# The state of an S5 branch: three elementwise operations that ran on POOL run on DVE

## The chip, the core and the metric

The kernel runs on one core of one Trainium2 chip. A core has a matrix engine (TensorE, here PE, with its weight loads as PEld), a vector engine (VectorE, DVE), a scalar engine (ScalarE, ACT), a general engine (GpSimd, POOL) and a sync engine whose queue issues most of the DMAs (SyncE, SP). Each engine runs its own queue of instructions in order and waits on semaphores of the others. The metric is the device time of one execution in microseconds, here the median of several runs. A profiled execution gives the trace; its times are from the start of its span.

## What is computed

One layer of a hybrid block on x of 1024 tokens by 1024 channels, in float32. After an RMSNorm, one combined projection makes the inputs of all branches. Branch A is the S5 state space: 64 groups of 16 channels with 64 complex states each. Branch B is sparse attention: an indexer scores the keys, each query keeps the 256 best, and attention runs over those. Both are gated and merged, then follow an output projection, a SwiGLU and a last norm. Cut to what matters here:

```python
lb_re = mag * jnp.cos(ai * dt)
lb_im = mag * jnp.sin(ai * dt)
...
x_re = f_re * bu_re - f_im * bu_im
x_im = f_re * bu_im + f_im * bu_re
a_s_re = jnp.broadcast_to(lb_re, shp)
a_s_im = jnp.broadcast_to(lb_im, shp)
...
_, _, h_re, h_im = lax.associative_scan(combine, (a_s_re, a_s_im, x_re, x_im), axis=0)
y = (jnp.einsum('lbgp,gcp->blgc', h_re, c_re.astype(f32))
     - jnp.einsum('lbgp,gcp->blgc', h_im, c_im.astype(f32))
     + d_skip.astype(f32) * uf)
```

## The kernel before

**Precision.** Matmuls run on float32 data split in a high and a low part (`whi`, `wlo`, `h_hi`, `h_lo`); a product is three matmuls (L209 to L211). So each weight tile needs a cast (L89, on ACT or, for most gate weights, POOL) and a subtraction on DVE (L90), and many results are split in the same way (L192, L193).

**S5 in chunks.** Time is cut in pieces of 8 steps, so 128 chunks. Within a chunk a Toeplitz matrix gives the output; between chunks only the state is carried. A complex rotation per chunk is taken out of the state beforehand, so that the rest is a real recurrence with a positive factor `r8`, which DVE's scan instruction runs along the 128 chunks. Afterwards the rotation is put back. `s5_batch` handles one of 8 batches of 8 groups; `s5_half` half a batch, so there are 16 halves. A half has 128 partitions (64 states, real parts above, imaginary below) and 4 groups x 128 chunks = 512 elements in each. Its steps:

- POOL makes `bt` and `ct` (L544 to L550), PE transposes `bt` into `s5t` (L554), ACT copies it into `ba` (L555), PE makes the Toeplitz blocks `s5k` (L558), and `kt` goes by DMA into `toep`.
- ACT makes the sines `sn` and cosines `cs` of the angles (L572, L573); POOL and DVE prepared the angles for both halves (`s5_angles`, L516 to L522).
- PE multiplies the input by `ba` into `s5a` (L577). DVE multiplies `s5a` by `cs` and `sn` (L579 to L581) into `a1` and `a2`, and POOL subtracts (L582): the rotated input. DVE scans (L584, four of them). DVE multiplies by `sn` (L586, L587), POOL by `cs` (L588) and adds (L589): the state.
- PE multiplies the state into `s5y` beside the Toeplitz part (L593, L594), ACT copies it out.

In the profile `a1` and `a2` both read `a`.

**What runs beside it.** The main loop is a list of projection jobs: indexer queries, queries, S5 inputs, values, gates. After each job the program takes 2 or 3 steps of S5, from the eighth job on 2 or 3 steps of the indexer scores (L356 to L359: PE, ACT, and DVE adding into `sc`), and from the twenty-second on the steps of the top-k search (`topk`). The search has 31 rounds: DVE makes `cand` (L633), ACT counts four of six segments (L637) and DVE two (L624), DVE makes `msk` (L641) and updates `bits` (L642), and the next round starts. After the search come the masks, the GLU and branch A, then attention, the output projection and the FFN.

**What sets the order.** The code is written engine by engine, but a scheduler of the framework places the instructions on the engines' queues by a simulated timeline, with the program order as priority. So moving an operation to another engine also shifts others. On the chip each queue runs strictly in its placed order.

**Buffers.** PSUM is 8 banks, four for `g` (projections, GLU) and four for `x` (S5 tiles and indexer scores alike), so an indexer score waits for a bank that may hold an S5 tile.

Of the kernel before, what the change touches and what calls it, by code (L numbers as in the profile page):

```python
# [54 lines left out]
def block_kernel(ctx, tc, xT, gv, wk, wfo, rope, s5s, s5b, s5c, ldt, dsk, cst, cm, out):  # L55
    nc = tc.nc
    V, S, G, PE, SP = nc.vector, nc.scalar, nc.gpsimd, nc.tensor, nc.sync
# [468 lines left out]
    def s5_half(b, hf, sp, U, ang):  # L526
        g0 = b * 8 + hf * 4
        gs = slice(g0, g0 + 4)
        MU, AD, SU = OP.mult, OP.add, OP.subtract
        gt = G.tensor_tensor  # L530
        W = [P, 4, P]

        def T(tag, bufs=1):
            return sp.tile(W, F32, tag=tag, name=tag, bufs=bufs)
        bco = lambda t, e0, n: t[:, gs, e0:e0 + n, None].to_broadcast([P, 4, n, 16])
        bb = sp.tile([P, 2, 4, 16], F32, tag="bb", name="bb")
        cc = sp.tile([P, 2, 4, 16], F32, tag="cc", name="cc")
        SP.dma_start(out=bb, in_=s5b[:, :, gs])
        SP.dma_start(out=cc, in_=s5c[:, :, gs])
        V.tensor_scalar(cc[64:, 0], cc[64:, 0], -1.0, None, op0=MU)  # L540
        bx = lambda t, j, n: t[:, j, :, None, :].to_broadcast([P, 4, n, 16])
        m2 = sp.tile([P, 4, 9, 16], F32, tag="m2", name="m2")
        bt = sp.tile([P, 4, 8, 16], F32, tag="bt", name="bt")
        gt(bt, bco(wfr, 0, 8), bx(bb, 0, 8), op=MU)  # L544
        gt(m2[:, :, :8], bco(wfs, 0, 8), bx(bb, 1, 8), op=MU)
        gt(bt, bt, m2[:, :, :8], op=AD)
        ct1 = sp.tile([P, 4, 9, 16], F32, tag="ct1", name="ct1", bufs=2)
        gt(ct1, bco(wr, 0, 9), bx(cc, 0, 9), op=MU)
        gt(m2, bco(wi, 0, 9), bx(cc, 1, 9), op=MU)
        gt(ct1, ct1, m2, op=SU)  # L550
        ba = T("ba", 2)
        pt = px.tile(W, F32, tag="x", name="s5t")
        for g in range(4):
            PE.transpose(pt[:, g], bt[:, g].rearrange("p s c -> p (s c)"), ident)  # L554
        S.copy(ba, pt)  # L555
        pk = px.tile(W, F32, tag="x", name="s5k")
        for g in range(4):
            PE.matmul(pk[:16, g], bt[:, g, 7], ct1[:, g, 0:8], start=True, stop=True)  # L558
        kt = sp.tile([16, 4, P], F32, tag="kt", name="kt")
        dd = sp.tile([16, 4, 16], F32, tag="dd", name="dd")  # L560
        V.tensor_tensor(dd, dk[:, gs, None].to_broadcast([16, 4, 16]),
                        ident[:16, None, :16].to_broadcast([16, 4, 16]), op=MU)
        S.copy(kt[:, :, 16:], pk[:16, :, 16:])
        V.tensor_tensor(kt[:, :, :16], pk[:16, :, :16], dd, op=AD)
        tp = toep[hf]
        for s_ in range(8):
            SP.dma_start(out=tp[16 * s_:16 * s_ + 16, :, 16 * s_:], in_=kt[:, :, :P - 16 * s_])
        yield
        sn, cs = T("sn"), T("cs")
        at_, ab = [t[64 * hf:64 * hf + 64] for t in ang]  # L570
        for o, sg in ((0, 1.0), (64, -1.0)):
            S.activation(sn[o:o + 64], at_, AF.Sin, scale=sg * TWO_PI_S)  # L572
            S.activation(cs[o:o + 64], ab, AF.Sin, scale=-TWO_PI_S, bias=hpi[64 * hf:64 * hf + 64])  # L573
        yield
        pa = px.tile(W, F32, tag="x", name="s5a")
        for g in range(4):
            PE.matmul(pa[:, g], ba[:, g], U[:, hf * 4 + g], start=True, stop=True)  # L577
        a1, a2 = T("a1", 2), T("a2")
        V.tensor_tensor(a1, pa, cs, op=MU)  # L579
        V.tensor_tensor(a2[:64], pa[64:], sn[64:], op=MU)  # L580
        V.tensor_tensor(a2[64:], pa[:64], sn[:64], op=MU)  # L581
        gt(a1, a1, a2, op=SU)  # L582
        for g in range(4):
            V.tensor_tensor_scan(a1[:, g], r8[:, g0 + g:g0 + g + 1].to_broadcast([P, P]), a1[:, g], 0.0,  # L584
                                 op0=MU, op1=AD)
        V.tensor_tensor(a2[:64], a1[64:], sn[64:], op=MU)  # L586
        V.tensor_tensor(a2[64:], a1[:64], sn[:64], op=MU)  # L587
        gt(a1, a1, cs, op=MU)  # L588
        gt(a1, a1, a2, op=AD)  # L589
        yield  # L590
        py = px.tile(W, F32, tag="x", name="s5y")
        for g in range(4):
            PE.matmul(py[:, g], tp[:, g], U[:, hf * 4 + g], start=True, stop=False)  # L593
            PE.matmul(py[:, g, 1:], ct1[:, g, 1:9], a1[:, g, :P - 1], start=False, stop=True)  # L594
        ys = sp.tile(W, F32, tag="ys", name="ys")
        S.copy(ys, py)
        SP.dma_start(out=yscr[b][:, hf * 4:hf * 4 + 4], in_=ys)
        yield

    def s5_batch(b, sp):  # L600
        U = sp.tile([P, 8, P], F32, tag="U", name="U", bufs=1)
        SP.dma_start(out=U, in_=uscr[b].rearrange("s (ci g) c -> (s ci) g c", g=8))
        ang = s5_angles(b, sp)
        yield
        for hf in range(2):
            yield from s5_half(b, hf, sp, U, ang)
# [503 lines left out]
    AD, SU = OP.add, OP.subtract  # L1110
# [261 lines left out]
```

## Time and profile before

| | us |
|---|---|
| median of 3 timed runs | 1870.43 |
| their lowest and highest | 1869.25, 1874.48 |
| the profiled execution | 1872.03 |
| its span, first to last instruction | 1870.1 |
| PE busy in the span | 1788.5 (96%) |
| DVE busy | 1356.6 (73%) |
| ACT busy | 885.4 (47%) |
| POOL busy | 657.8 (35%) |

The granted TensorE clock is 0.982 of full speed on average over the span. S5 runs from about 145 to 640 us, the indexer scores from about 200 to 515, the search from about 520 to 735, the masks to 790, the first attention scores come at 812. Busy shares over the whole span mix stages with different limits, so they are read by stretch. "Idle before, releaser" names what ended an engine's wait, by the last semaphore that came.

### The profile page before, as it was taken

What the parts mean: (1) busy time and instruction counts of PE and PEld (TensorE: products, weight loads), DVE (VectorE), ACT (ScalarE), POOL (GpSimd) and SP (SyncE); (2) the same over time, 40 slices, a digit from 0 to 9 for tenths busy, and PEclk for the clock granted to TensorE, in tenths of its full rate; (3) what the DMA queues carried; (4) which work ended last, traced back from release to release, by engine and by line L of the source; (5) the groups of instructions that cost most, each with busy time, mean ns of one, the idle gap of its engine ahead of it and who ended that gap; (6) DMA issues with size and microseconds to landing.
All of it is one profiled execution on the core that took longest, in us unless ns stands there. A gap on an engine that the chain in (4) does not pass through costs nothing.

```text
span 1870.1 us, 23523 instructions
## 1 busy us (share of the span) xinstructions
PE 1788.5 (96%) x8334; PEld 1476.8 (79%) x8334; DVE 1356.6 (73%) x2230; ACT 885.4 (47%) x1460; POOL 657.8 (35%) x471
## 2 busy tenths in 40 slices
PE   7999999989888999999999999999999999999996
PEld 6888788868676777778887778878888888888885
DVE  6966566675798878966668666787676766679876
ACT  5333345464556886155667645632323232343344
POOL 5158415263566321200000001356656656400013
PEclk9999999999999999999999999999999999999998
DMA  4464444333222342162337465422121222295432
GB/s 175 141 208 142 139 133 136 102 111 99 86 72 96 105 135 68 68 214 102 114 105 243 158 213 188 161 91 102 68 94 76 90 79 79 79 351 207 151 124 90
DMA packets 149077, 243.03 MB, mean 130 GB/s; under 512 B 26976, under 2 KB 79200, under 8 KB 148960
## 3 DMA queue, kind: packets, MB, share of 16 engines
q1 hardware_dynamic: 146336, 238.33, 38.0%
q10 hardware_dynamic: 2624, 3.20, 0.5%
q8 instruction: 66, 1.08, 0.2%
q14 instruction: 51, 0.42, 0.1%
HBM read 172.02 MB, written 66.06 MB: 127 GB/s over the span
## 4 chain that ended last, share of the span: by engine, by line
PE 64%; DVE 12%; ACT 6%; DMA 5%; issue 3%; POOL 2%; SPq 0%; DVEq 0%; ACTq 0%; POOLq 0%
PE pm L846 7%; PE pm L845 7%; PE pm L844 7%; PE g L694 4%; PE g L696 4%; PE g L695 4%; PE g L209 3%; PE g L210 3%; PE g L211 3%; PE pm L1155 3%; PE pm L1154 3%; PE pm L1153 3%; ACT junk L637 3%; PE pt L760 2%; PE ips L356 1%
## 5 line engine op out<-in xcount | busy, mean ns | idle before, releaser
L209 PE MATMUL g<-h_hi,whi 128*128 128x512 f32 (+1 forms) x704 | 276.0, 393 | 7.7 <-ACT whi L89 6.9
L211 PE MATMUL g<-h_hi,wlo 128*128 128x512 f32 (+1 forms) x704 | 275.7, 392 | 4.2 <-DVE wlo L90 4.2
L210 PE MATMUL g<-h_lo,whi 128*128 128x512 f32 (+1 forms) x704 | 275.4, 391 | 1.6 <-DVE h_lo L158 1.6
L209 PEld LDWEIGHTS g<-h_hi,whi 128*128 128x128 f32 x704 | 134.6, 191 | 33.5 <-ACT whi L89 6.9
L211 PEld LDWEIGHTS g<-h_hi,wlo 128*128 128x128 f32 x704 | 134.6, 191 | 30.4 <-DVE wlo L90 5.8
L210 PEld LDWEIGHTS g<-h_lo,whi 128*128 128x128 f32 x704 | 134.6, 191 | 27.5 <-DVE h_lo L158 3.0
L90 DVE TENSOR_TENSOR wlo<-raw,whi 128x1024 fp32r<-128x1024 f32 x93 | 127.2, 1368 | 23.9 <-ACT whi L89 22.0
L359 DVE SCALAR_TENSOR_TENSOR sc<-ips,wq,sc 128x384 f32<-128x384 f32 (+3 forms) x160 | 99.7, 651 | 57.6 <-ACT ips L358 56.5
L358 ACT ACTIVATE ips<-ips,rqi 128x384 f32<-128x384 f32 (+3 forms) x160 | 90.0, 588 | 85.7 <-PE ips L357 77.8
L89 POOL CAST whi<-raw 128x1024 fp32r<-128x1024 f32 x28 | 37.3, 1332 | 222.9 <-PE g L695 129.7
L637 ACT ACTIVATE junk<-sc,cand 128x384 bf16<-128x384 f32 (+1 forms) x124 | 96.2, 776 | 37.9 <-DVE cand L633 35.7
L89 ACT CAST whi<-raw 128x1024 fp32r<-128x1024 f32 x65 | 68.3, 1051 | 80.4 <-issue 15.9
L846 PE MATMUL pm<-c,wlo 128*128 128x512 f32 x264 | 102.9, 390 | 2.2 <-DVE wlo L193 2.2
L844 PE MATMUL pm<-c,whi 128*128 128x512 f32 x264 | 102.7, 389 | 0.0
L845 PE MATMUL pm<-c,whi 128*128 128x512 f32 x264 | 102.7, 389 | 0.0
L193 DVE TENSOR_TENSOR wlo<-s,whi 128x512 fp32r<-128x512 f32 x88 | 93.7, 1086 | 3.5 <-ACT whi L192 3.5
L870 POOL TENSOR_TENSOR gate<-gate,rb 128x512 f32<-128x512 f32 x44 | 67.9, 1543 | 79.5 <-DVE gate L853 79.5
L1023 POOL TENSOR_TENSOR xg<-xg 128x512 f32<-128x512 f32 x4 | 7.1, 1784 | 234.5 <-ACT xg L808 234.5
L873 DVE TENSOR_TENSOR hid<-hid,gate 128x512 f32<-128x512 f32 x44 | 53.8, 1222 | 47.4 <-POOL gate L872 47.4
L192 ACT CAST whi<-s 128x512 fp32r<-128x512 f32 x88 | 52.5, 621 | 65.3 <-PE pm L845 61.2
L624 DVE TENSOR_SCALAR_CACHE_REDUCE junk<-sc,cand 128x896 bf16<-128x896 f32 (+1 forms) x62 | 75.1, 1211 | 1.9
L871 ACT ACTIVATE gate<-gate 128x512 f32<-128x512 f32 x44 | 27.9, 633 | 97.7 <-POOL gate L870 97.7
(383 smaller groups left out, 5158.4 us busy)
## 6 DMA issues: line engine op xcount, KB each, us to landing
raw<-in_wk SPq DMA_DIRECT2D x95, 512.0 KB, 4.1
raw<-in_wfo SPq DMA_DIRECT2D x41, 512.0 KB, 3.6
hscr<-hid SPq DMA_DIRECT2D x22, 512.0 KB, 2.6
ra<-in_wk SPq DMA_DIRECT2D x21, 512.0 KB, 3.1
rw<-in_wk SPq DMA_DIRECT2D x21, 512.0 KB, 3.1
gscr<-go SPq DMA_DIRECT2D x16, 512.0 KB, 4.8
q<-qscr SPq DMA_DIRECT2D x16, 512.0 KB, 5.1
st<-qiscr SPq DMA_DIRECT2D x16, 384.0 KB, 3.3
```

The source lines that it names most:

```text
L89: (eng or S.copy)(hi[:, :kt], raw[:, :kt])
L90: V.tensor_tensor(lo[:, :kt], raw[:, :kt], r32(hi[:, :kt]), op=OP.subtract)
L193: V.tensor_tensor(lo, src, r32(hi), op=OP.subtract)
L209: PE.matmul(ps, hi[:, k], act[0][:, k, c], start=(k == 0), stop=False)
L210: PE.matmul(ps, hi[:, k], act[1][:, k, c], start=False, stop=False)
L211: PE.matmul(ps, lo[:, k], act[0][:, k, c], start=False, stop=(k == KT - 1))
L358: S.activation(ps, ps, AF.Relu, scale=rqi[:, i:i + 1])
L359: V.scalar_tensor_tensor(seg(i)[:, c], ps, wq[:, i - 2, h:h + 1], seg(i)[:, c], op0=OP.mult, op1=OP.add)
L637: S.activation(junk2[:, :n], seg(j + 2), AF.Sign, bias=cand.bitcast(F32)[:, j:j + 1], scale=-1.0, accum_out=cnt[:, j:j + 1])
L844: PE.matmul(ps, hi[:, k], b[:, k], start=(k == 0), stop=False)
L845: PE.matmul(ps, hi[:, k], b[:, 4 + k], start=False, stop=False)
L846: PE.matmul(ps, lo[:, k], b[:, k], start=False, stop=(k == 3))
```

## The change

In `s5_half`, L582, L588 and L589 are issued on DVE in place of POOL. `gt` is `G.tensor_tensor`, POOL's form of the same instruction, and `V` is DVE; operands and results are the same. There are 16 halves, so 48 instructions leave POOL's queue (476 instructions before, 428 after) and 48 join DVE's (2154, 2202). PE, ACT and SP have the same instructions as before, in a shifted order: the S5 steps of the last halves stand earlier among the matmuls (the first `s5a` of the last half at place 2459 in PE's queue, 2521 before), and from the output projection on PE's order is the same.

```diff
--- before.py
+++ after.py
@@ -579,14 +579,14 @@
         V.tensor_tensor(a1, pa, cs, op=MU)
         V.tensor_tensor(a2[:64], pa[64:], sn[64:], op=MU)
         V.tensor_tensor(a2[64:], pa[:64], sn[:64], op=MU)
-        gt(a1, a1, a2, op=SU)
+        V.tensor_tensor(a1, a1, a2, op=SU)
         for g in range(4):
             V.tensor_tensor_scan(a1[:, g], r8[:, g0 + g:g0 + g + 1].to_broadcast([P, P]), a1[:, g], 0.0,
                                  op0=MU, op1=AD)
         V.tensor_tensor(a2[:64], a1[64:], sn[64:], op=MU)
         V.tensor_tensor(a2[64:], a1[:64], sn[:64], op=MU)
-        gt(a1, a1, cs, op=MU)
-        gt(a1, a1, a2, op=AD)
+        V.tensor_tensor(a1, a1, cs, op=MU)
+        V.tensor_tensor(a1, a1, a2, op=AD)
         yield
         py = px.tile(W, F32, tag="x", name="s5y")
         for g in range(4):
```

DVE's queue beside the indexer scores, in the eleventh half (L579 to L581 the first products, L584 the scans, L359 the scores). Before:

```order
L359 SCALAR_TENSOR_TENSOR sc<-ips,wq,sc 128x384
L561 TENSOR_TENSOR dd<-dk,ident 16x64
L359 SCALAR_TENSOR_TENSOR sc<-ips,wq,sc 128x384
L584 SCALAR_TENSOR_TENSOR a_4028<-r_138,a_4028 128x128 x4
L359 SCALAR_TENSOR_TENSOR sc<-ips,wq,sc 128x448 x2
L586 TENSOR_TENSOR a_4029<-a_4028,sn 64x512
L587 TENSOR_TENSOR a_4029<-a_4028,sn 64x512
L359 SCALAR_TENSOR_TENSOR sc<-ips,wq,sc 128x512 x2
L359 SCALAR_TENSOR_TENSOR sc<-ips,wq,sc 128x384
```

Now:

```order
L359 SCALAR_TENSOR_TENSOR sc<-ips,wq,sc 128x384
L582 TENSOR_TENSOR a_4028<-a_4028,a_4029 128x512
L561 TENSOR_TENSOR dd<-dk,ident 16x64
L359 SCALAR_TENSOR_TENSOR sc<-ips,wq,sc 128x384
L584 SCALAR_TENSOR_TENSOR a_4028<-r_138,a_4028 128x128 x4
L359 SCALAR_TENSOR_TENSOR sc<-ips,wq,sc 128x448 x2
L586 TENSOR_TENSOR a_4029<-a_4028,sn 64x512
L587 TENSOR_TENSOR a_4029<-a_4028,sn 64x512
L359 SCALAR_TENSOR_TENSOR sc<-ips,wq,sc 128x512
L588 TENSOR_TENSOR a_4028<-a_4028,cs 128x512
L359 SCALAR_TENSOR_TENSOR sc<-ips,wq,sc 128x512
L589 TENSOR_TENSOR a_4028<-a_4028,a_4029 128x512
```

L582, L588 and L589 stand among the score additions L359, one ahead of the second and two between those that follow L587.

DVE's queue in a round of the search, with the fourteenth half in it (a_4740 is `a1`, a_4741 is `a2`). Before:

```order
L641 TENSOR_TENSOR msk<-cnt,lim 128x6
L584 SCALAR_TENSOR_TENSOR a_4740<-r_138,a_4740 128x128 x4
L642 COPY_PREDICATED bits<-msk,cand 128x6
L586 TENSOR_TENSOR a_4741<-a_4740,sn 64x512
L587 TENSOR_TENSOR a_4741<-a_4740,sn 64x512
L633 TENSOR_SCALAR cand<-bits 128x6
L624 TENSOR_SCALAR junk,cnt<-sc,cand 128x896
L624 TENSOR_SCALAR junk,cnt<-sc,cand 128x1024
```

Now:

```order
L641 TENSOR_TENSOR msk<-cnt,lim 128x6
L582 TENSOR_TENSOR a_4740<-a_4740,a_4741 128x512
L642 COPY_PREDICATED bits<-msk,cand 128x6
L584 SCALAR_TENSOR_TENSOR a_4740<-r_138,a_4740 128x128 x2
L633 TENSOR_SCALAR cand<-bits 128x6
L584 SCALAR_TENSOR_TENSOR a_4740<-r_138,a_4740 128x128 x2
L624 TENSOR_SCALAR junk,cnt<-sc,cand 128x896
L586 TENSOR_TENSOR a_4741<-a_4740,sn 64x512
L587 TENSOR_TENSOR a_4741<-a_4740,sn 64x512
L624 TENSOR_SCALAR junk,cnt<-sc,cand 128x1024
```

Between `msk` and the next `cand` now stand an L582 and two of the scans; L586 and L587 have moved behind `cand`.

POOL's queue in the eleventh and the angles of the seventh batch (t_ are the angles, ct_ and bt of the next half). Before:

```order
L544 TENSOR_TENSOR bt<-wfr,bb 128x512
L582 TENSOR_TENSOR a_4028<-a_4028,a_4029 128x512
L588 TENSOR_TENSOR a_4028<-a_4028,cs 128x512
L516 TENSOR_TENSOR t_4385<-cvec,qh 128x512
L589 TENSOR_TENSOR a_4028<-a_4028,a_4029 128x512
L517 TENSOR_TENSOR t_4386<-cvec,ql 128x512
L518 TENSOR_TENSOR t_4387<-t_4385,t_4386 128x512
L520 TENSOR_TENSOR t_4385<-t_4385,t_4387 128x512
```

Now:

```order
L544 TENSOR_TENSOR bt<-wfr,bb 128x512
L516 TENSOR_TENSOR t_4385<-cvec,qh 128x512
L517 TENSOR_TENSOR t_4386<-cvec,ql 128x512
L518 TENSOR_TENSOR t_4387<-t_4385,t_4386 128x512
L520 TENSOR_TENSOR t_4385<-t_4385,t_4387 128x512
L548 TENSOR_TENSOR ct_4406<-wr,cc 128x576
L521 TENSOR_TENSOR t_4385<-t_4385,t_4386 128x512
```

The three operations, which wait for DVE, no longer stand ahead of the angles and of `ct`.

## Rows read from the trace of the kernel before

**Rows 1.** Busy us by stretch: stretch, length, engines with instruction counts, PEclk, DMA.

```profile
140.00:400.00 260.00, 256.07 (x1296) 215.17 (x1296) 168.51 (x253) 118.01 (x195) 121.41 (x94) 0.99 0.44 128
400.00:515.00 115.00, 104.63 (x497) 83.13 (x495) 80.72 (x130) 55.62 (x99) 60.84 (x48) 0.96 0.32 97
515.00:640.00 125.00, 108.93 (x511) 87.00 (x512) 105.24 (x175) 82.93 (x174) 71.00 (x51) 0.95 0.29 92
640.00:720.00 80.00, 73.32 (x297) 58.17 (x297) 60.12 (x108) 71.12 (x133) 20.62 (x12) 0.94 0.37 115
720.00:800.00 80.00, 79.26 (x340) 63.42 (x339) 76.43 (x132) 23.85 (x46) 15.46 (x7) 1.00 0.16 60
```

**Rows 2.** Busy us of a 20 us stretch, columns as in rows 1.

```profile
480.00:500.00 20.00, 14.54 (x76) 11.46 (x76) 17.99 (x36) 12.09 (x23) 9.93 (x9) 0.83 0.19 56
```

**Rows 3.** Waits of PE, 400 to 720 us: in total, times, longest.

```profile
PE s5a L577 <- ACT ba L555: 9.2, 3, 5.6
PE ips L356 <- DVE sc L359: 4.8, 5, 1.6
...
PE ips L356 <- DVE a L581: 2.0, 2, 1.2
PE s5y L594 <- POOL a L589: 1.9, 2, 1.1
PE s5t L554 <- POOL bt L546: 1.2, 1, 1.2
```

**Rows 4.** Timeline, 488 to 492 us: start, length, engine, line, idle before.

```profile
488.25 1.24 DVE L359 SCALAR_TENSOR_TENSOR sc<-ips,wq,sc 128x448 f32<-128x448 f32 x2
...
489.52 0.69 DVE L586 TENSOR_TENSOR a<-a,sn 64x512 f32<-64x512 f32 x1
...
491.74 0.79 PE L356 MATMUL ips<-ki,st 128*128 128x512 f32 x1 [1.58 <-DVE sc L359]
```

**Rows 5.** POOL groups of the three operations: busy, mean ns, idle before them.

```profile
L582 POOL TENSOR_TENSOR a<-a,a 128x512 f32<-128x512 f32 x16 | 21.9, 1368 | 77.0 <-DVE a L581 77.0
L589 POOL TENSOR_TENSOR a<-a,a 128x512 f32<-128x512 f32 x16 | 21.5, 1343 | 0.5
L588 POOL TENSOR_TENSOR a<-a,cs 128x512 f32<-128x512 f32 x16 | 20.6, 1290 | 56.8 <-DVE a L587 53.8 <-ACT whi L89 3.0
```

**Rows 6.** Timeline of DVE, operations that follow one another.

```profile
720.91 0.68 DVE L680 TENSOR_TENSOR yt<-y_hi,y_lo 128x512 f32<-128x512 f32 x1
721.51 0.16 DVE L641 TENSOR_TENSOR msk<-cnt,lim 128x6 int32<-128x6 f32 x1
...
725.51 0.69 DVE L680 TENSOR_TENSOR yt<-y_hi,y_lo 128x512 f32<-128x512 f32 x1
726.31 0.69 DVE L681 TENSOR_TENSOR yt<-yt,sg 128x512 f32<-128x512 f32 x1
```

**Rows 7.** DVE groups of the search, 515 to 640 us.

```profile
L641 DVE TENSOR_TENSOR msk<-cnt,lim 128x6 int32<-128x6 f32 x16 | 10.1, 634 | 16.9 <-ACT junk L637 16.7
L633 DVE TENSOR_SCALAR cand<-bits 128x6 int32<-128x6 int32 x16 | 9.0, 561 | 0.5
L642 DVE COPY_PREDICATED bits<-msk,cand 128x6 int32<-128x6 int32 x16 | 7.4, 463 | 0.5
```

**Rows 8.** Timeline, one round of the search beside POOL.

```profile
571.11 1.26 POOL L589 TENSOR_TENSOR a<-a,a 128x512 f32<-128x512 f32 x1
...
571.36 1.04 DVE L641 TENSOR_TENSOR msk<-cnt,lim 128x6 int32<-128x6 f32 x1 [1.20 <-ACT junk L637]
572.33 2.36 POOL L326 TENSOR_TENSOR go<-go,rb 128x1024 f32<-128x1024 f32 x1
...
572.43 2.29 DVE L642 COPY_PREDICATED bits<-msk,cand 128x6 int32<-128x6 int32 x1
```

**Rows 9.** DVE group of L587, 140 to 650 us.

```profile
L587 DVE TENSOR_TENSOR a<-a,sn 64x512 f32<-64x512 f32 x16 | 12.1, 755 | 0.2
```

**Rows 10.** Timeline of PE, first matmul of branch A.

```profile
792.32 0.47 PE L694 MATMUL g<-ya_hi,whi 128*128 128x512 f32 x1 [0.74 <-ACT sg L679]
```

## The prediction, written before the changed kernel had run

> **What bounds the kernel now.** Read the busy times by stretch first [rows 1], since only the stretches up to about 720 us hold work that the change touches. TensorE (PE) is busy 256.1 of 260 us from 140 to 400, so there it is the bound and nothing beside it counts. From 400 to 515 it is busy 104.6 of 115, from 515 to 640 108.9 of 125, from 640 to 720 73.3 of 80: these 33 us of idle time are where a change to DVE or POOL can show, in either direction. The same rows carry the granted clock: 0.96, 0.95 and 0.94 in these three stretches, against 0.99 before, so an idle PE is paid for twice. One 20 us window shows the second price: clock 0.83 [rows 2], so about a third of it ran at 1.2 instead of 2.4 GHz and half of that, 3.3 us, was lost beside the idle time itself.
>
> Next, whom PE waits for between 400 and 720 [rows 3]. The reader is to see that POOL is named for little: 1.9 us for the state (`a`, L589) and 1.2 us for `bt`. Most of the time is lost to the ACT copy `ba` (9.2 us) and to DVE (`sc` 4.8 us, `a` 2.0 us). The waits of `ips` for `sc` come in bursts: PE needs a PSUM buffer that DVE frees only after its S5 steps, as around 488 us, where two `sc` (1.24 us) are followed by the S5 steps, and PE waits 1.58 us for a buffer [rows 4].
>
> Last, the three operations themselves. On POOL they are 16 of each, 21.9 + 20.6 + 21.5 = 64.0 us [rows 5]. POOL waits 77.0 us for L581 and 53.8 us for L587, with everything queued behind: the angles, `bt` and `ct` of the next half, the weight casts. In 515:640 the top-k search runs too, a loop between DVE (`msk`, `bits`, `cand`) and ACT (`junk`). Its three small DVE operations take 0.16 us when nothing is in the way (L641 in [rows 6]), and 0.63, 0.56 and 0.46 us on average in this stretch [rows 7]. Why is seen at 571 us: `msk` takes 1.04 us while POOL is in L589, `bits` 2.29 us while POOL is in L326 [rows 8]. The Trainium skill (GPSIMD Engine Reference, section Specifications) says that POOL shares its SBUF interfaces with VectorE, and that the two get in each other's way where the DVE instruction has two SBUF inputs or a 2-port mode. The trace agrees, and by that rule the moved operations, which have two SBUF inputs, are themselves exposed to the POOL work that stays.
>
> **The price of a moved operation.** The nearest row is L587, two SBUF inputs and 512 elements a partition: 755 ns on average over the S5 stretch, collisions with POOL included [rows 9]. One undisturbed is 0.69 us (489.52 in [rows 4]). An operation that needs the result of the one in front starts 0.80 us after it (725.51 to 726.31); one that doesn't starts 0.60 us after it (720.91 to 721.51) [rows 6]. I take 0.75 us, with 0.69 and 0.80 as ends: 48 x 0.75 = 36 us more on DVE, 64 us less on POOL. The Trainium skill (VectorE: DVE Perf Modes, section "The DRAIN you can't avoid") says that a semaphore after each DVE operation costs nothing extra. The rows say 0.2 us, so the measurement decides; by the page the 48 would be 33 us instead of up to 38.
>
> **Part by part, against the profiled execution's own 1872.0 us (span 1870.1).**
> - 140 to 400 us, eight halves, 24 operations, 18 us of DVE time. DVE is busy 168.5 of 260 us and PE 98.5% [rows 1]: hidden under the matmuls, 0. If the cover were gone it could cost about as much as PE's idle time there once more, 4 us; it can win at most those 4 us. The value taken is 0, because PE has next to nothing to lose or win there.
> - 400 to 515 us, four halves less the end of the last, 11 operations. Two of the halves stand in bursts in which PE waits for `sc`. In the new order one moved operation stands ahead of the burst's later `sc` in the first, and three stand between them in the second. Four operations on PE's path: 4 x 0.75 = +3.0 us. Ends: 0 (ACT, not DVE, is the later one), and all eleven, +8 us. I stay near the order's count.
> - 515 to 640 us, the last four halves and one operation of the half before, 13 operations: 13 x 0.75 = 9.8 us more on DVE. Against it stands what the search gets back: `msk`, `cand` and `bits` lose (0.634 + 0.561 + 0.463 - 3 x 0.16) x 16 = 18.8 us to collisions [rows 7]. POOL is busy 121.4 + 60.8 + 71.0 = 253.2 us from 140 to 640 [rows 1], 64.0 of it with the moved operations, a quarter: 4.7 us come back. Net 5.1 us on DVE. Part of it falls into DVE's 16.7 us of waiting for `junk` [rows 7] and costs nothing; but in four rounds of the new order an L582 and two or four scans stand between `msk` and `cand`, in the loop's serial part, where the old order has scans in one round. I take two thirds, +3.5 us. Ends: -4.7 (all new work sheltered) and +9.8 (none, nothing given back). A later end of the search is not forgiven afterwards: at 792 us PE already waits 0.74 us for ACT's `sg` to free a PSUM buffer [rows 10], and DVE is busy 76.4 of 80 us from 720 to 800 [rows 1].
> - POOL's own lateness goes: PE no longer waits for L589, and `bt` no longer stands behind it: 1.9 + 1.2 = -3.1 us [rows 3]. Ends: 0 and -3.1. What is late next at these places is DVE's L589, behind `junk` counts of the search.
> - The last halves move up: the last `s5a` stands 62 PE instructions earlier. PE waits 9.2 us for `ba`, an ACT copy queued among the search's `junk` operations, and the copy is no faster than it was. Taken as 0; ends -9.2 us with one cold stretch of 3.3 us, and as much the other way, since PE's order now asks for the last halves sooner than DVE and ACT may deliver them.
>
> Sum: 3.0 + 3.5 - 3.1 = +3.4 us, so 1875.4 us for an execution like the profiled one. That one lies 1.6 us above the median of the three timed runs (1870.4, from 1869.3 to 1874.5); on the median's footing it is **1873.8 us**.
>
> **Rivals.**
> *DVE becomes the bound (slower).* Place: the search's loop in 515:640, where DVE is busy 105.2 of 125 us. If `cand` is what ACT waits for in nearly every round, the full 9.8 us lands on the loop, the bursts cost 3.0, and one more cold stretch 3.3, less POOL's 3.1: +13.0 us, 1883 us. It decides once DVE is later than ACT at `msk`, that is once DVE's waits for `junk` (16.7 us now) are nearly gone. For it: DVE is fuller than ACT there (105.2 against 82.9 us). Against: those 16.7 us, and the collisions that go.
>
> *POOL's queue was the hidden bound (faster).* With POOL never blocked behind L581 and L587, the next half's preparations are ready early, the last halves leave the search's stretch sooner, half of the 9.2 us for `ba` and a cold stretch (3.3) go, and 3.1 and 4.7 come back, with the bursts' 3.0 still paid: 4.6 + 3.3 + 3.1 + 4.7 - 3.0 = -12.7 us, 1858 us on the median's footing; with the loop's new work half exposed (+5), 1863 us. For it: the moved-up halves in the order, and 130 us of POOL waits. Against: [rows 3] name POOL for 3.1 us only.
>
> *It does nothing to the end.* All new DVE work is covered, and POOL's relief too: 1870 us. This is the lower half of the middle case.
>
> **How the numbers follow.** The middle case (within -2 and +8 us of the median) has 0.50, DVE as the bound 0.28, POOL as the hidden bound 0.22. A difference under 0.3% (5.6 us, 1864.8 to 1876.0) can't be told from none here. The upper part of the middle case lies beyond it: slower is 0.28 + 0.05 = 0.33, within is 0.45, faster 0.22. The middle case's own range is 1868 to 1879; the range for 8 in 10 reaches to most of both rivals, 1861 to 1886.
>
> **What would show it.** Right: the moved operations at 0.69 to 0.80 us on DVE; DVE busy time up by 25 to 36 us and POOL's down by 64; the means of `msk`, `bits` and `cand` in the search lower; no PE wait for POOL's `a`; PE's waits for `sc` in the two bursts longer by some 3 us; 140 to 400 us unchanged. Wrong: a PE idle time from 400 to 720 that changes by more than 8 us in sum, above all at `ba`; DVE's waits for `junk` gone (the slower rival), or the search ending earlier against the matmuls (the faster one); a change after 800 us, where I expect none.

## The result, and the profile after

The changed kernel takes 1881.99 us (median of 7 runs, 1877.35 to 1885.05), the kernel before 1871.01 us beside it (7 runs, 1869.25 to 1874.48). The ratio is 1.0051, 95% interval 1.0040 to 1.0062: 9.5 us slower, where 3.4 us and "no change that can be measured" had been the likeliest. The ratio is taken from all runs together; it is not the quotient of the two medians, which lie 11.0 us apart. The profiled execution took 1885.05 us, span 1883.1, granted clock 0.976 (before 0.982).

The stretches of [rows 1] again, same columns:

```profile
140.00:400.00 260.00, 254.69 (x1275) 212.68 (x1274) 179.86 (x275) 115.32 (x192) 88.12 (x69) 0.99 0.44 127
400.00:515.00 115.00, 106.45 (x499) 84.66 (x498) 87.36 (x135) 56.06 (x98) 52.96 (x39) 0.91 0.33 99
515.00:640.00 125.00, 108.72 (x504) 88.40 (x504) 111.68 (x184) 80.09 (x163) 52.26 (x35) 0.92 0.26 81
640.00:720.00 80.00, 72.27 (x295) 56.62 (x296) 58.62 (x107) 67.56 (x128) 22.64 (x12) 0.96 0.44 132
720.00:800.00 80.00, 80.00 (x345) 64.27 (x344) 78.56 (x137) 27.98 (x58) 11.25 (x7) 1.00 0.14 47
```

POOL gave up its work (121.4 to 88.1 us in the first stretch, 657.8 to 595.8 over the span) and DVE took it (168.5 to 179.9, 80.7 to 87.4, 105.2 to 111.7). PE's idle time from 400 to 720 us hardly changed (33.1 us before, 32.6 now), but its clock fell: 0.96 to 0.91 from 400 to 515, 0.95 to 0.92 from 515 to 640. The 20 us of [rows 2] have it at 0.74 in place of 0.83. Whom PE waits for between 400 and 720 us, beside [rows 3]:

```profile
PE s5y L594 <- DVE a L589: 11.6, 3, 7.0
PE ips L356 <- DVE sc L359: 6.7, 7, 2.9
...
PE ips L356 <- DVE a L581: 2.5, 2, 1.4
...
PE s5a L577 <- ACT ba L555: 0.4, 1, 0.4
```

The wait for ACT's `ba` is gone (9.2 to 0.4 us), where the last halves now stand among other matmuls in PE's queue. In its place stands a wait that the kernel before hardly had: `s5y` for the state, 1.9 us on POOL before, 11.6 us on DVE now. With the stretch from 140 to 400 us it is 15.4 us in five waits. The longest, in the trace of the changed kernel (start, length, engine, line, idle before):

```profile
564.09 2.65 DVE L586 TENSOR_TENSOR a<-a,sn 64x512 f32<-64x512 f32 x1
566.75 1.66 DVE L587 TENSOR_TENSOR a<-a,sn 64x512 f32<-64x512 f32 x1
568.44 1.28 DVE L624 TENSOR_SCALAR_CACHE_REDUCE junk<-sc,cand 128x1024 bf16<-128x1024 f32 x1
...
569.64 1.54 DVE L522 TENSOR_SCALAR t<-t 128x512 f32<-128x512 f32 x1
571.11 1.54 DVE L588 TENSOR_TENSOR a<-a,cs 128x512 f32<-128x512 f32 x1
...
572.68 0.69 DVE L589 TENSOR_TENSOR a<-a,a 128x512 f32<-128x512 f32 x1
```

```profile
563.78 2.41 POOL L326 TENSOR_TENSOR go<-go,rb 128x1024 f32<-128x1024 f32 x1 [1.05 <-ACT go L325]
566.15 1.71 POOL L546 TENSOR_TENSOR bt<-bt,m 128x512 f32<-128x512 f32 x1
...
570.98 1.11 POOL L545 TENSOR_TENSOR m<-wfs,bb 128x512 f32<-128x512 f32 x1
```

```profile
573.43 0.79 PE L594 MATMUL s5y<-a,ct 128*128 128x127 f32 x2 [7.03 <-DVE a L589]
```

Read it from the end. PE stands still for 7.03 us until L589 (0.69 us) is done. L589 is last in a row of DVE work that includes a count of the search (L624) and an angle operation of another half (L522), and three DVE operations run into POOL's: L586 takes 2.65 us in place of 0.69 beside L326, L587 1.66 beside L546, L588 1.54 beside L545. On DVE the moved operations are in line with all this; on POOL they were in line with nothing of the search.

The moved operations by group over the S5 stretch, and the search's three small ones from 515 to 640 us, beside [rows 5, 7]:

```profile
L589 DVE TENSOR_TENSOR a<-a,a 128x512 f32<-128x512 f32 x16 | 15.6, 973 | 0.1
L588 DVE TENSOR_TENSOR a<-a,cs 128x512 f32<-128x512 f32 x16 | 14.9, 931 | 0.1
...
L582 DVE TENSOR_TENSOR a<-a,a 128x512 f32<-128x512 f32 x16 | 12.9, 804 | 0.1
```

```profile
L642 DVE COPY_PREDICATED bits<-msk,cand 128x6 int32<-128x6 int32 x13 | 6.4, 491 | 0.2
...
L633 DVE TENSOR_SCALAR cand<-bits 128x6 int32<-128x6 int32 x14 | 5.2, 375 | 0.3
...
L641 DVE TENSOR_TENSOR msk<-cnt,lim 128x6 int32<-128x6 f32 x14 | 4.2, 299 | 5.3 <-ACT junk L637 5.1
```

The means of `msk` and `cand` fell (634 to 299, 561 to 375 ns), that of `bits` did not (463 to 491). But only 14 rounds fit into the stretch in place of 16, and DVE's wait for ACT's `junk` is down from 16.7 to 5.1 us: DVE has become the later one. The first `msk` of the search starts at 532.8 us, 526.6 before, the last at 742.7 us, 732.2 before: of the 10.5 us by which the search ends later, 6.2 are there when it begins. Branch A's first matmul comes at 796.5 us, 792.3 before, the first scores at 818.5 (812.0), the first FFN matmul at 1224.3 (1211.4). So of the 13 us between the two profiled executions 4 are there when branch A starts and 6.5 at the first scores; the other half comes behind them, where no moved operation runs. The first 60 us of attention, before and after (columns as in [rows 1]):

```profile
812.00:872.00 60.00, 56.71 (x269) 46.16 (x268) 37.14 (x99) 39.53 (x54) 2.09 (x2) 0.97 0.47 162
```

```profile
818.50:878.50 60.00, 53.59 (x241) 43.19 (x240) 34.23 (x95) 37.76 (x52) 2.08 (x2) 0.91 0.48 164
```

PE is idle 6.4 us there in place of 3.3, and the clock is 0.91 in place of 0.97. Its waits there, of which the one for `th` is new:

```profile
PE sps L736 <- DVE mx L739: 3.2, 2, 2.5
PE po L772 <- ACT th L192: 2.8, 1, 2.8
```

### The profile page after: what moved, and what is told of

The parts are those of the page before. It is cut to its first block, busy times and chain, and to the rows that moved or that the text cites. A ratio compares the mean times of both kernels' runs of the same rounds, so it can differ in the third digit from the quotient of the medians.

```text
span 1883.1 us, 23514 instructions
## 1 busy us (share of the span) xinstructions
PE 1798.1 (95%) x8334; PEld 1483.7 (79%) x8334; DVE 1388.2 (74%) x2278; ACT 884.8 (47%) x1460; POOL 595.8 (32%) x423
## 4 chain that ended last, share of the span: by engine, by line
PE 63%; DVE 14%; DMA 6%; ACT 4%; issue 4%; POOL 2%; SPq 1%; DVEq 0%; ACTq 0%; POOLq 0%
PE pm L846 7%; PE pm L844 7%; PE pm L845 7%; PE g L696 4%; PE g L694 4%; PE g L695 4%; PE pm L1155 3%; PE pm L1153 3%; PE pm L1154 3%; PE g L209 3%; PE g L211 3%; PE g L210 3%; DVE junk L624 1%; PE ips L356 1%; PE pt L760 1%
## 5 line engine op out<-in xcount | busy, mean ns | idle before, releaser
L359 DVE SCALAR_TENSOR_TENSOR sc<-ips,wq,sc 128x384 f32<-128x384 f32 (+3 forms) x160 | 99.9, 652 | 47.8 <-ACT ips L358 47.1
L624 DVE TENSOR_SCALAR_CACHE_REDUCE junk<-sc,cand 128x896 bf16<-128x896 f32 (+1 forms) x62 | 75.0, 1210 | 1.6
```

The lines of the kernel that those rows point to most:

```text
L359: V.scalar_tensor_tensor(seg(i)[:, c], ps, wq[:, i - 2, h:h + 1], seg(i)[:, c], op0=OP.mult, op1=OP.add)
L624: V.tensor_scalar(junk[:, :n], seg(j + 2), t[:, j:j + 1], None, op0=op, op1=OP.add, accum_out=cnt[:, j:j + 1])
```

## The experiments

Two things changed at once: the engine of 48 operations, and the order in which the scheduler put everything else. So most runs hold the order fixed: an order-only dependency from each instruction to the next ties every engine's queue to a list, that of the kernel before or that of the changed kernel. `PE_before` and the like stand for lists of instructions in queue order; the loop is always this:

```diff
+    for q in order:
+        for x, y in zip(q, q[1:]):
+            tc.add_manual_dep(made[y], x, nosync, reason="order")
```

Differences in us are (ratio - 1) x 1871. All runs are against the kernel before on the same chip.

| run | the three operations | order | ratio (95%) | us |
|---|---|---|---|---|
| the change | DVE | its own | 1.0051 (1.0040 to 1.0062) | +9.5 |
| e1 | DVE | before | 1.0034 (1.0021 to 1.0046) | +6.4 |
| e2 | POOL | after | 1.0049 (1.0034 to 1.0064) | +9.2 |
| e3 | DVE, 1 of 128 columns | before | 0.9971 (0.9960 to 0.9982) | -5.4 |
| e4 | POOL, and idle ones on DVE | before | 1.0121 (1.0105 to 1.0137) | +22.6 |
| e5 | DVE | after, from branch A on before | 1.0022 (1.0008 to 1.0036) | +4.1 |
| e6 | POOL | before, from branch A on after | 1.0013 (1.0001 to 1.0025) | +2.4 |
| e7 | DVE in the first 8 halves | before | 1.0003 (0.9990 to 1.0016) | +0.6 |
| e8 | DVE in the last 8 halves | before | 1.0042 (1.0028 to 1.0056) | +7.9 |
| e9 | DVE | after, from the GLU on before | 1.0041 (1.0030 to 1.0053) | +7.7 |
| e10 | POOL | before, from the GLU on after | 1.0025 (1.0013 to 1.0037) | +4.7 |
| e11 | L582 on DVE | before | 1.0021 (1.0011 to 1.0031) | +3.9 |
| e12 | L588, L589 on DVE | before | 1.0045 (1.0029 to 1.0061) | +8.4 |

**e1: the change in the order of the kernel before.**

```diff
-        gt(a1, a1, a2, op=SU)
+        V.tensor_tensor(a1, a1, a2, op=SU)
...
-        gt(a1, a1, cs, op=MU)
-        gt(a1, a1, a2, op=AD)
+        V.tensor_tensor(a1, a1, cs, op=MU)
+        V.tensor_tensor(a1, a1, a2, op=AD)
...
+    order = [PE_before, DVE_before_with_the_48, ACT_before, SP_before, POOL_before_without_the_48]
```

> The three operations are on DVE as in the changed kernel, but the instructions of every engine are held in the order of the kernel before (L582 stands on DVE right before its scan, L588 and L589 right behind L587; nothing else moves). Theory 1, the fuller DVE queue (25 to 36 us more of DVE work between 400 and 640 us, PE waits for L589): the loss of 11 us is still there, 1879 to 1883 us against 1871 before. Theory 2, the other order that the scheduler chose (last halves of S5 earlier on PE, other order of attention and branch A): the loss is gone, 1870 to 1873 us. In between, about 1876: half of it by each.

Measured 1879.83 us, +6.4 us: two thirds of the loss, so theory 1 holds the larger part here but not all. Most of it is there when branch A starts (first matmul at 798.2 us against 792.3); from there to the first FFN matmul it takes 419.9 us against 419.1. Where it comes from is seen in two ways. The first is whom PE waits for from 400 to 720 us. Before, beside [rows 3]:

```profile
PE pv L336 <- DVE sc L359: 2.1, 2, 1.5
...
PE s5t L554 <- DVE sc L359: 1.2, 2, 0.9
```

And in this run:

```profile
PE ips L356 <- DVE sc L359: 7.1, 5, 2.5
PE s5t L554 <- POOL bt L546: 5.8, 1, 5.8
PE s5a L577 <- ACT ba L555: 5.0, 2, 3.6
...
PE s5t L554 <- DVE sc L359: 3.9, 1, 3.9
PE pv L336 <- DVE sc L359: 3.3, 2, 2.8
PE s5y L594 <- DVE a L589: 2.2, 1, 2.2
```

The waits for the scores `sc`, at whatever matmul, grow from 8.1 to 14.3 us, by about as much as the whole loss. Those for `bt` and `ba` together hardly change (10.4 and 10.8 us), nor do those for the state (1.9 and 2.2). How a moved operation reaches PE is seen in one burst of scores of this run, beside the same burst in [rows 4]:

```profile
490.84 0.68 DVE L587 TENSOR_TENSOR a<-a,sn 64x512 f32<-64x512 f32 x1
491.56 0.69 DVE L588 TENSOR_TENSOR a<-a,cs 128x512 f32<-128x512 f32 x1
492.29 0.69 DVE L589 TENSOR_TENSOR a<-a,a 128x512 f32<-128x512 f32 x1
492.90 1.93 DVE L359 SCALAR_TENSOR_TENSOR sc<-ips,wq,sc 128x512 f32<-128x512 f32 x3
...
493.70 0.80 PE L356 MATMUL ips<-ki,st 128*128 128x512 f32 x1 [2.52 <-DVE sc L359]
```

L588 and L589 stand between L587 and the next scores, and PE waits 2.52 us for its PSUM buffer in place of 1.58. The second way: PE's queue has the same order in both kernels, so one and the same matmul can be compared. Four of them, before:

```profile
402.88 0.39 PE L356 MATMUL ips<-ki,st 128*128 128x320 f32 x1 [1.17 <-DVE a L581]
...
515.68 0.63 PE L554 MATMUL s5t<-ident,bt 128*128 128x128 f32 x4 [0.90 <-DVE sc L359]
...
575.96 0.66 PE L554 MATMUL s5t<-ident,bt 128*128 128x128 f32 x4 [1.25 <-POOL bt L546]
...
587.60 2.08 PE L577 MATMUL s5a<-U,ba 128*128 128x128 f32 x8 [5.61 <-ACT ba L555]
```

And in this run:

```profile
400.84 0.39 PE L356 MATMUL ips<-ki,st 128*128 128x320 f32 x1 [1.16 <-DVE a L581]
...
520.74 1.06 PE L554 MATMUL s5t<-ident,bt 128*128 128x128 f32 x4 [3.91 <-DVE sc L359]
...
584.01 1.11 PE L554 MATMUL s5t<-ident,bt 128*128 128x128 f32 x4 [5.75 <-POOL bt L546]
...
592.39 1.16 PE L577 MATMUL s5a<-U,ba 128*128 128x128 f32 x8
```

The first comes 2.0 us earlier than before, the second, behind the last burst, 5.1 us later: 7.1 us are lost beside the scores. Beside the search, the third is 8.1 us late, behind a wait of 5.75 us for `bt`; but the fourth is only 4.8 us late, since the wait of 5.61 us for `ba` that stood there before is gone. The last `msk` of the search comes 5.6 us late (737.8 against 732.2). So the search hands on the delay of the scores and adds some 0.5 us to it. These are single profiled executions, and e7 below, whose moved operations all lie ahead of 400 us, shows how far two of them differ by themselves: from the last scores to the last `msk` the distance to the kernel before changes by 0.9 us.

**e2: the kernel before in the order of the changed one.**

```diff
+    order = [PE_after, DVE_after_without_the_48, ACT_after, SP_after]
```

> The three operations are on POOL as in the kernel before, but PE, DVE, ACT and SP are held in the order of the changed kernel. Theory 1 (fuller DVE queue): 1870 to 1873 us. Theory 2 (the other order): 1879 to 1883 us. In between, about 1876, if half of the loss is the order.

Measured 1882.93 us, +9.2 us: by this run theory 2. It is no clean price of the order, though. POOL's queue was left to the scheduler, and the order was laid out for a state made by DVE, and with POOL it asks for `s5y` too early, a single wait of 6.5 us among them:

```profile
PE s5y L594 <- POOL a L589: 13.7, 4, 6.5
```

Read the other way it is clear: in the order of the changed kernel no difference can be measured between the engines that do the three operations (+9.2, interval 6.4 to 12.0, and +9.5 us, 7.5 to 11.6). In the order of before it makes 6.4 us. The effects do not add, so both theories hold a part.

**e3: POOL relieved, DVE hardly loaded.**

```diff
-        V.tensor_tensor(a1, a1, a2, op=SU)
+        V.tensor_tensor(a1[:, :, :1], a1[:, :, :1], a2[:, :, :1], op=SU)
...
-        V.tensor_tensor(a1, a1, cs, op=MU)
-        V.tensor_tensor(a1, a1, a2, op=AD)
+        V.tensor_tensor(a1[:, :, :1], a1[:, :, :1], cs[:, :, :1], op=MU)
+        V.tensor_tensor(a1[:, :, :1], a1[:, :, :1], a2[:, :, :1], op=AD)
...
+    order = [PE_before, DVE_before_with_the_48, ACT_before, SP_before, POOL_before_without_the_48]
```

> As the first run, but the three operations on DVE treat only one of the 128 columns of each of their four groups (the state's other columns stay unfinished), so that DVE has almost nothing more to do and POOL is relieved all the same; the order of the kernel before. Theory 1: with DVE's added time gone the loss is gone, and POOL's relief shows: 3 us of PE's waits for POOL and 5 us of collisions back, 1863 to 1870 us. Theory 2: 1870 to 1871, since the order is that of before. If POOL's relief is worth nothing: 1871.

Measured 1867.84 us, -5.4 us, as theory 1 has it. The one group of this run and of e1 that compare best:

```profile
L588 DVE TENSOR_TENSOR a<-a,cs 128x4 f32<-128x4 f32 x16 | 2.7, 169 | 0.6
```

```profile
L588 DVE TENSOR_TENSOR a<-a,cs 128x512 f32<-128x512 f32 x16 | 11.1, 693 | 0.6
```

The order and POOL's relief are the same in e1 and e3; what differs is DVE's time in the three groups, 35.7 us in e1 and 9.0 in e3. Those 26.7 us cost 6.4 + 5.4 = 11.8 us. So POOL's relief is worth 5.4 us or a little more, and about four tenths of the DVE time comes back as kernel time. (The thin operations also finish the state sooner; no run tells that apart from POOL's relief.) The traces say where. From the matmul that stands at 402.88 us before to the last scores, this run loses 2.3 us and e1 7.1; from there to the last `msk` this run gains 3.5 us and e1 loses 0.5. So by these single traces DVE's time costs some 4 to 5 us in each of the two stretches, and POOL's relief makes up for it beside the search, not beside the scores. The search has the same wait of PE for `bt` here as in e1, though this kernel is faster than the one before:

```profile
PE s5t L554 <- POOL bt L546: 5.4, 1, 5.4
```

That wait is therefore not the price of the moved operations.

**e4: the load without the relief.**

```diff
-        gt(a1, a1, a2, op=SU)
+        zz.append(V.tensor_tensor(z, cs, cs, op=MU).ins.name); gt(a1, a1, a2, op=SU)
...
-        gt(a1, a1, cs, op=MU)
-        gt(a1, a1, a2, op=AD)
+        zz.append(V.tensor_tensor(z, cs, cs, op=MU).ins.name); gt(a1, a1, cs, op=MU)
+        zz.append(V.tensor_tensor(z, cs, cs, op=MU).ins.name); gt(a1, a1, a2, op=AD)
...
+    order = [PE_before, DVE_before_with_the_48_idle_ones, ACT_before, SP_before, POOL_before]
```

> The kernel before in its own order, POOL does its three operations, and DVE does beside them three idle multiplies of the same 128x512 form at the same places, on whose result nothing waits. If DVE's load alone is the cause: 1876 to 1883 us. If it is that PE waits for L589 at the end of DVE's queue: 1871 to 1873. Theory 2 (the order): 1871 to 1872.

(`z` is a bf16 tile of its own; `zz` collects the names for the order.) Measured 1895.03 us, +22.6 us, above each range it was given: more work on DVE is enough to make the kernel slower, with nobody waiting for its results. The size is not the price of the load alone, though. The idle groups take 50.4 us (26.6 + 12.7 + 11.1), but DVE and POOL work on the state at the same time here, and POOL's L588 takes 1.73 us on average in place of 1.29. PE's wait for the state, made by POOL, grows from 1.9 to 7.6 us, beside 14.3 us for `sc` (7.2 + 3.7 + 3.4), as in e1:

```profile
PE s5y L594 <- POOL a L589: 7.6, 2, 5.7
```

That 22.6 of 50.4 is 0.45, near the 0.44 of e1 and e3 (11.8 of 26.7), is therefore no confirmation. The idle multiply at L589 shows the collision:

```profile
L589 DVE TENSOR_TENSOR z<-cs 128x512 bf16<-128x512 f32 x16 | 26.6, 1660 | 0.5
...
L588 DVE TENSOR_TENSOR z<-cs 128x512 bf16<-128x512 f32 x16 | 11.1, 693 | 0.5
```

The same operation with the same operands takes 0.69 us on average at L588 and 1.66 at L589, where POOL's L588 runs beside it.

**e7 and e8: the first and the last eight halves.**

```diff
-        gt = G.tensor_tensor
+        gt = G.tensor_tensor; vt = V.tensor_tensor if b < 4 else gt
...
-        gt(a1, a1, a2, op=SU)
+        vt(a1, a1, a2, op=SU)
...
-        gt(a1, a1, cs, op=MU)
-        gt(a1, a1, a2, op=AD)
+        vt(a1, a1, cs, op=MU)
+        vt(a1, a1, a2, op=AD)
```

e8 has `b >= 4`; both hold the order of before.

> The three operations on DVE in the first eight halves alone (24 of the 48, those that ran between 140 and 400 us), the order of the kernel before. If the forecast's zero for this stretch is right: 1870 to 1874 us. If the 6 us of the first run were spread evenly over the operations: 1875. If POOL's relief alone counts here, since PE covers DVE: 1867 to 1870.

> The three operations on DVE in the last eight halves alone (24 of the 48, those between 400 and 640 us), the order of the kernel before. If the loss of the first run belongs to the stretch in which PE follows the search and the scores: 1877 to 1880 us. If spread evenly: 1875. If it is the first halves' lateness that is carried forward: 1871 to 1873.

Measured 1872.06 us (+0.6) and 1878.99 us (+7.9). The whole loss of e1 is in the last eight halves, where the scores and the search run. In e8 PE waits for `sc` as long as in e1 (14.3 us), and between the matmul that stands at 402.88 us before and the last scores it loses the same 7.1 us; in e7 PE waits 5.8 us for `sc` and loses nothing there. Where PE is the bound, 24 more operations on DVE cost nothing that can be measured.

**e11 and e12: by operation.** e11 puts only L582 on DVE, e12 only L588 and L589, each in the order of before (the diff of e1, a part each).

> Only the subtraction L582 on DVE, L588 and L589 stay on POOL; the order of the kernel before. All three cost 6.4 us in this order. If each operation costs the same: 2 us, 1873. If L582 is the costly one, since it now stands in front of the scans in DVE's queue: 1875 to 1877. If it is free, since DVE waited there for POOL anyway: 1869 to 1871.

> Only L588 and L589 on DVE, L582 stays on POOL; the order of the kernel before. If each operation costs the same: 4 us, 1875. If these two are the costly ones, since they lengthen DVE's queue where a wait for POOL was not in its way: 1876 to 1879. If L582 is the costly one: 1871 to 1873.

Measured 1872.62 us (+3.9) and 1875.66 us (+8.4) against 1868.98 us for the kernel before in that session. No single operation is the cause, but the way is not the same: PE waits 14.6 us for `sc` in e12, as in e1, and 6.2 in e11, where its wait for the state on POOL grows instead, from 1.9 to 5.0 us. So L588 and L589 lengthen the waits for the scores. The two losses together are 12.3 us, 5.9 more than the 6.4 of all three, while the three intervals together explain 4.2. A reason that was only read from the profiles: half moved, POOL still waits for DVE in the middle of its queue (61.6 us for L587 in e11, 21.2 us for L581 in e12, 400 to 660 us), so the load is paid and little of the relief comes.

**e5, e6, e9, e10: where the other order costs.** The program is cut in two by the order in which it was written, and each engine follows one list for what is ahead of the cut and another for what is behind. e5 and e6 cut at branch A:

```diff
+    order = [e_after_up_to_branch_A for e in engines] + [e_before_from_branch_A for e in engines]
```

(e6: before and after exchanged, on the kernel before.)

> The changed kernel, in its own order up to the GLU, but attention, branch A and all that follows are held in the order of the kernel before on each engine. Theory A (the order of attention's first 60 us, with PE's waits for th and a clock of 0.71 there, costs 7 to 9 us by itself): the ratio to before falls from 1.0051 to about 1.001 to 1.0025, 1874 to 1877 us. Theory B (attention loses because the search and the GLU before it end later and leave other work open): 1880 to 1883 us, as in the changed kernel.

> The kernel before, in its own order up to the GLU, with the three operations on POOL; only attention, branch A and what follows are held in the order of the changed kernel. Theory A: 7 to 9 us slower than before, 1879 to 1881 us, with the first scores at the same time as before (812 us) and PE waiting 2.8 us for th behind them. Theory B: 1871 to 1873 us.

Measured 1875.93 us (+4.1) and 1873.05 us (+2.4). e5 falls as theory A has it, e6 rises by a third of what theory A has. So they were repeated with a cut at the first GLU instruction, by the same edit:

> The changed kernel, each engine in its own order up to the first GLU instruction (about 695 us), and from there on (GLU, rest of the search, attention, branches, FFN) in the order of the kernel before, cut sharply. Theory A (the order behind 695 us costs by itself): the stretch from the first branch A matmul to the first FFN matmul is back to 418 to 421 us from 428, the whole 1872 to 1875 us. Theory B (that stretch is longer because the search ends later): 425 us or more for the stretch, 1878 to 1882 us. The earlier hybrid, cut at branch A, had 424.

> The kernel before, each engine in its own order up to the first GLU instruction, and from there on in the order of the changed kernel, cut sharply. Theory A: 425 to 428 us from the first branch A matmul to the first FFN matmul (419 before), 1876 to 1880 us. Theory B: 419 us and 1871 us. The earlier hybrid, cut at branch A, had 422 us and was 2.4 us slower.

Measured 1876.97 us (+7.7) and 1874.32 us (+4.7). The stretch from branch A's first matmul to the first FFN matmul is 420.3 us in e9 (427.8 in the changed kernel), as theory A expects; its branch A starts late, at 798.4 us, so that the whole misses theory A's 1875. In the mirror, the profiled execution of e10, the stretch is 419.8 us, where theory A wanted 425 to 428. What differs between e10 and the changed kernel there is not the order and not the idle time:

```profile
812.60:872.60 60.00, 53.71 (x254) 43.39 (x253) 36.42 (x98) 38.70 (x54) 2.10 (x2) 0.97 0.47 160
```

PE is idle 6.3 us in these 60 us, as in the changed kernel (6.4), at a clock of 0.97 in place of 0.91. That execution of e10 took 1871.23 us, less than its median of 1874.32, so its profile need not show what the runs lose. With the other order from the GLU on, PE is idle some 3 us longer in these 60 us (e2 5.9 us, e10 and the change 6.3 and 6.4, against 3.2 to 3.6 in before, e1, e3, e4, e7, e8, e9, e11 and e12). The two kernels cut at branch A lie between (e6 4.9, e5 4.7 us). What the clock adds to it differs from execution to execution. By the timed runs this order costs 2.4 us (0.2 to 4.7, e6) and 4.7 us (2.4 to 6.9, e10), and taking it away from the changed kernel gives back 5.4 us (e5) and 1.8 us (e9, not clear of the two intervals).

**What is settled and what is open.** Shown: in the order of before, DVE's longer queue costs time only beside the scores and the search (e7, e8), and it reaches PE through the waits for `sc` (8.1 us before, 14.3 in e1, 14.3 to 14.6 in e8, e12 and e4). Beside the search POOL's relief makes up for it; this is read from one trace each of e1 and e3. Shown as well: the scheduler's other order behind the GLU costs by itself, some 2 to 5 us. Open is how the other order of the S5 stretch and DVE's load share the remaining 4 to 8 us of the changed kernel, since the two do not add. In that kernel PE's waits in the S5 stretch are others than in e1: 11.6 us for the state and 6.7 for `sc`. No version that does all of the work beats the kernel before; e7 is level with it.

## Why the prediction was right and where it failed

Its range of 25 us held the time, its likeliest case did not: 1873.8 us forecast, 1882.0 measured, and slower, to which it gave 0.33. That the measured time lies near the slower rival's 1883 is luck: e1 does not find the loss in the search's loop, and 2 to 5 us of it have a cause that no rival named.

- *The price of a moved operation* (0.75 us) was right in the order of before: 35.7 us for 48 in e1, 36 forecast. In e1's burst L589, which needs L588, starts 0.73 us after it, where 0.80 had been taken for such a pair. In the changed kernel they take 43.4 us, 0.80 to 0.97 us each on average: 12 of the 48 last until a POOL operation ends, 3 in e1.
- *140 to 400 us, 0* was right in the order of before: +0.6 us (-1.9 to 3.0) in e7.
- *400 to 515 us, +3.0 through the `sc` bursts* had the right wait in the order of before and less than half of its size: e1 and e8 lose 7.1 us there, with three bursts and three moved operations in each, where four in two bursts had been counted. In the changed kernel's own order PE's waits for `sc` fell in this stretch from 4.8 to 3.9 us; what got worse there is the clock (0.96 to 0.91).
- *515 to 640 us, +3.5*, less 3.1 for POOL, was near in the order of before: 0.4 us forecast for the stretch, 0.5 us from the last scores to the last `msk` in e1. (Two thirds of 5.1 are 3.4, not 3.5.) In all, steps two to four were to cost 3.0 + 3.5 - 3.1 = 3.4 us, and e8 measured 7.9 (5.2 to 10.5): what is missing is beside the scores. The relief was sized well (3.1 + two thirds of 4.7 = 6.2 us; e3 5.4), the load too small: 9.5 us forecast, 11.8 between e1 and e3. A round of the loop is indeed longer where operations stand between `msk` and `cand` (7.9 us in place of 4.0 in the round that begins at 568 us in e1), but the delay is soon made up: the `msk` behind that round is 8.3 us late, the next one 4.4, as late as the one ahead of it (4.5).
- *POOL's lateness goes, -3.1* failed. PE's wait for the state went from 1.9 to 11.6 us in that stretch, and in e1 it is still 2.2. The prediction named the successor itself ("what is late next at these places is DVE's L589, behind `junk` counts of the search") and put no price on it. A wait that is named as the next one needs its own term.
- *The last halves, `ba`, 0 with 9.2 us to each side*: the wait did go, 8.8 us of it, and the same earlier order brought the waits for L589 instead. The two about cancel, so the sum was near, for no good reason.
- *Nothing after 800 us* failed: 2 to 5 us there by order alone (e5, e6, e9, e10). The comparison of the orders had shown that PE's order is shifted up to the output projection; it was read as if only the S5 steps mattered.
- *The slower rival* was half right. Its sign came, `junk` waits from 16.7 to 5.1 us, and the search ended 10.5 us later by its last `msk`; but 6.2 us of these were there at its first, and in e1 the search adds 0.5. Its price, 13 us, is above the 6.4 of e1 and near the whole loss only with the other order's cost added.
- *The faster rival* had a real mechanism, POOL's relief, at 5.4 us in place of 12.7, and DVE's load outweighs it.
- *Of the signs*, DVE's and POOL's busy times came (+31.6 and -62.0 us). The mean of `bits` did not fall, the waits for `sc` did not grow, and PE's idle time from 400 to 720 us changed by 0.6 us only, so that this sign did not see the loss.
- The rule of the Trainium skill on contention (GPSIMD Engine Reference, section Specifications) did speak against the change: by it the moved operations are exposed to the POOL work that stays. The changed kernel's trace agrees, L588 1.54 us beside POOL where it takes 0.69 alone (e1), and so do the two rows of e4.

## What to carry to other kernels

An operation that moves to a fuller queue costs by its place: ask what stands behind it in that queue, and which engine waits for that (here the scores, whose PSUM buffers PE waits for). A longer wait in a trace is not yet a loss: compare one and the same instruction further on, and see whether a later wait has become shorter by as much, as `ba` has behind `bt`. Where a scheduler places the queues, a local edit is two changes, and the second can cost as much as the first; tie the order down before crediting a difference to the edit. Compare idle time and granted clock apart from each other: one execution's clock is no evidence on the order.

## What the runs showed of the hardware

- Executions of one program differ by as much as this effect, and the slower ones show the lower clock: the 12 runs of e10 go from 1868.58 us at 0.986 to 1879.44 us at 0.980, the 7 of the changed kernel from 1877.35 us at 0.982 to 1885.05 us at 0.976. In the profiles, 6.3 and 6.4 us of idle time within 60 us came with clocks of 0.97 and 0.91.
- Two DVE operations alike in everything but the moment took 0.69 and 1.66 us on average (e4, L588 and L589), by what POOL did beside them. A 64x512 product of 0.69 us took 2.65 us beside POOL's L326.
- In these cases the DVE operation does not run slower, it ends at a fixed time after POOL's. L586 above ends 0.55 us after L326 (566.74 and 566.19), L587 and L588 0.55 and 0.56 us after L546 and L545. All 16 idle multiplies at L589 in e4 end 0.55 us after POOL's L588, and the small `msk` and `bits` of [rows 8] 0.03 us after L589 and L326. L580 and L581, which read `s5a` from PSUM, never take more than 0.70 us in the changed kernel, though 8 of the 32 start while a POOL operation runs.
